# Context projections from undivided fp32 weights and state, and the squares of x summed by ScalarE along its rows

## The chip, the cores and the metric

The kernel runs on one core of a Trainium2 chip. The metric is the time of one execution on the device in microseconds (us), and runs are compared by their medians. A core has a matrix engine (TensorE, in the views PE, with its weight loads as PEld), VectorE (DVE), ScalarE (ACT), GpSimd (POOL) and SyncE (SP), whose queue issues most DMA transfers. Each engine works through its own instructions in order.

## The reference

One layer of a diffusion backbone with 1024 latent tokens and 256 context tokens of width 1024, batch 1. Both streams are normalised and modulated, then projected by the same weights. Of the context only what the latents need is wanted: the forget gates and values of the recurrence, from which its two end states `s_f` and `s_b` come, and the keys and values of two attentions.

```
m_lat = (silu(c) @ w_mod + b_mod).reshape(N_MOD, D);  m_ctx = (silu(c_ctx) @ w_mod + b_mod).reshape(N_MOD, D)
h_lat = rms_norm(x, norm_mix) * (1.0 + m_lat[1]) + m_lat[0]
h_ctx = rms_norm(ctx, norm_mix) * (1.0 + m_ctx[1]) + m_ctx[0]
aq, ak, av, bq, bk, bv, cq, cf, cb, ci, cg, gates = features(h_lat, w_in, qn_b, kn_b, rope)
caq, cak, cav, cbq, cbk, cbv, ccq, ccf, ccb, cci, ccg, cgates = features(h_ctx, w_in, qn_b, kn_b, None)
yc_ctx, s_f, s_b = hgrn2_bidir(ccq, ccf, ccb, cci, ccg, lb_f, lb_b, gn_c, s0, s0)
yc = hgrn2_bidir(cq, cf, cb, ci, cg, lb_f, lb_b, gn_c, s_f, s_b)[0]
ya = window_attn(aq, ak, av, cak, cav, sink_a);  yb = global_attn(bq, bk, bv, cbk, cbv)
x_mix = x + m_lat[2] * merge_branches(ya, yb, yc, gates, w_branch, w_out)
h = rms_norm(x_mix, norm_ffn) * (1.0 + m_lat[4]) + m_lat[3]
out = rms_norm(x_mix + m_lat[5] * conv_ffn(h, w_up, w_dw, b_dw, w_down), norm_final)
```

## The kernel before

The state is kept with channels on the 128 partitions, in KT = 8 tiles of 128 channels. A matmul of full precision is made of three in the format fp32r: a weight tile and a state tile are each divided into a high part (`wh`, `hh`) and a low part (`wl`, `hl`), and `wh*hh + wh*hl + wl*hh` is summed. `w_unit` loads a weight tile of 512 KB into `wr` (SP), casts it to `wh` (ACT) and subtracts to `wl` (DVE, or POOL for the tiles in `CTX_POOL`). Each of these three has three buffers.

The stages are: modulation, context, latent projections of the recurrence (`hgrn_head`, four heads), projections for two attentions, the attentions, and the FFN. This case is about the first 140 us.

*Modulation.* The scale and shift of both streams come in eight groups of 128 channels, each from a tile `wm` of 1 MB. For six groups PE multiplies (`pr`, 8 matmuls with two weight columns, L320), ACT copies the result to `row` and PE turns it (`pm`). Groups 1 and 4 (`MOD_OFF`) are summed on DVE in `acc` (L311, L314). When a group is done, the context tile of the same channels is scaled (`cx`, L252) and divided into `chh` and `chl` (L253, L254). So `ctx_h` runs group by group, and `CTX_K` sets the order of the eight channel tiles inside a context matmul.

*Context.* `ctx_c` makes, for each of four heads, two forget gates (`czf`, `czb`, with `forget` on ACT and DVE into `cF` and `cK`) and the values (`czv`, copied, transposed and copied again into `cV`). `ctx_kv` makes keys and values (`ckv`) of both attentions, with a head norm (`hrsc`) for the second. Beside it runs `lat_norm`: it loads x (`xT`, channels on partitions), squares it on ACT (L369), adds the squares over the channel tiles on POOL and DVE (`xss`), turns the sum on PE (`rcx`, `rms_r`), raises it to -1/2 on POOL (L237), spreads it on PE (`rpx`, `rms_bc`) and finishes the eight latent tiles (`finish_h`: L252 on DVE, L253 on ACT into `hh`, L254 on DVE into `hl`). `weave` puts the steps of the two generators in turn.

*State.* A tree of eight levels multiplies `cK` by the gates from its far side (L452, direction 0 on DVE, direction 1 on POOL by `TREE_POOL`), with the products of neighbours in between (L455). Then PE turns `cK` (`ckp`) and multiplies it by `cV` (`cu`). The first latent projection, `zq`, and the second, `zf`, follow on PE.

The order on each engine is set by a list scheduler at build time from the priorities in the code, so it is a result of the program and not written by hand.

Of the kernel before, what the change touches and what calls it, by code (L numbers as in the profile page):

```python
# [49 lines left out]
NORMAT = 3  # L50
TREE_POOL = (1,)

MOD_OFF = (1, 4)
MOD_FIN = {3: (1,), 6: (4,)}
CTX_K = (0, 2, 1, 3, 5, 4, 6, 7)

# [35 lines left out]
def build(tc, ins, out, dbg=None):  # L92
    nc = tc.nc
    V, A, G, T, SP = nc.vector, nc.scalar, nc.gpsimd, nc.tensor, nc.sync
    with ExitStack() as top:
# [84 lines left out]

        def gemm_cm(psl, w, h, cols, k0=0, c0=0, nk=None, first=True, last=True, order=None):

            wh, wl = w
            hh, hl = h
            nk = nk or wh.shape[1]
            c = slice(c0, c0 + P)
            for n, k in enumerate(order or range(nk)):
                s = first and n == 0
                e = last and n == nk - 1
# [19 lines left out]
        def rms_r(pool, parts, n, name, on_pe):  # L209
# [8 lines left out]
            if on_pe:  # L218

                pc = turned(f"rc{name}")  # L220
                for t in range(nt):
                    for j, ss in enumerate(parts):
                        T.matmul(pc[:, t], ss[:, t * P:(t + 1) * P], ident, start=j == 0, stop=j == len(parts) - 1)
                V.reduce_sum(out=r, in_=pc, axis=AX.X)
            else:
                for g, ss in enumerate(parts):
                    pc = turned(f"rc{name}{g}")
                    for t in range(nt):
                        T.transpose(pc[:, t], ss[:, t * P:(t + 1) * P], ident)
                    if g == 0:  # L230
                        V.reduce_sum(out=r, in_=pc, axis=AX.X)
                    else:
                        r2 = pool.tile([P, nt], F32, tag="rs2", name=f"rs2{name}{g}")
                        V.reduce_sum(out=r2, in_=pc, axis=AX.X)
                        V.tensor_tensor(out=r, in0=r, in1=r2, op=ALU.add)
            V.tensor_scalar(out=r, in0=r, scalar1=1.0 / D, scalar2=EPS, op0=ALU.mult, op1=ALU.add)
            G.tensor_tensor(out=r, in0=r, in1=mhalf[:, :nt], op=ALU.pow)  # L237
            return r
# [17 lines left out]
        with ExitStack() as s0:  # L256
            xp = Aligned(s0.enter_context(tc.tile_pool(name="xp", bufs=1, side="right", reuse_waits="tile")))
            chh = xp.tile([P, KT, LC], F32R, tag="chh", name="chh")
            chl = xp.tile([P, KT, LC], F32R, tag="chl", name="chl")
            xin = s0.enter_context(ExitStack())  # L260
# [5 lines left out]

            hc = (chh, chl)
            units0 = []
# [92 lines left out]
            def lat_norm():  # L361

                xss = [xq.tile([P, L], F32, tag=f"xss{i}", name=f"xss{i}") for i in range(2)]
                for k in range(4):
                    for i in range(2):
                        SP.dma_start(x32[:, 4 * i + k], ins["xT"][(4 * i + k) * P:(4 * i + k + 1) * P, :])
                        xk = x32[:, 4 * i + k]
                        sq = xss[i] if k == 0 else xq.tile([P, L], F32, tag=f"sq{i}", name=f"sqx{k}{i}")
                        A.activation(sq, xk, AF.Square)  # L369
                        if k > 0:  # L370
                            (G if i == 0 else V).tensor_tensor(out=xss[i], in0=xss[i], in1=sq, op=ALU.add)
                    yield
                V.tensor_tensor(out=xss[1], in0=xss[1], in1=xss[0], op=ALU.add)
                rl = rms_row(xq, xss[1:], L, "x")
                yield
                for k in range(KT):
                    finish_h(x32[:, k], rl, a01[:, k, 0:1], m01[:, k, 0, 0:1], hh[:, k], hl[:, k])
                    yield
# [11 lines left out]
            def ctx_unit(nm, h):  # L390
                if units0:
                    return units0.pop(0)
                return w_unit(ins["w_cm"][U_C[nm] + h], KT, P, G if (nm, h) in CTX_POOL else V)

            def ctx_c():
                for h in range(CH):
                    for d, nm in ((0, "f"), (1, "b")):
                        w = ctx_unit(nm, h)
                        z = bank("b", f"cz{nm}{h}", (P, LC))
                        gemm_cm(z, w, hc, slice(0, LC), order=CTX_K)  # L400
                        forget(nc, cp, z, cF[:, d, h], cK[:, d, h], lb[:, d * 4 + h:d * 4 + h + 1],
                               oml[:, d * 4 + h:d * 4 + h + 1], LC, f"c{nm}{h}")
# [42 lines left out]
            while B < LC:  # L445
# [1055 lines left out]
```

## Time and profile before

| | |
|---|---|
| time, median of 3 runs | 2192.55 us (2187.08 to 2196.15) |
| profiled execution | 2193.44 us, its span 2191.7 us |
| busy: PE, PEld, DVE, ACT, POOL | 96%, 79%, 67%, 46%, 20% of the span |
| chain that ended last | PE 22%, DVE 1%, of the span |
| moved by DMA | 224.60 MB, a mean of 102 GB/s |

The span runs from the first to the last instruction; the time of the execution has 1.7 us more around it. Busy shares are means over a long program with stages of different limits, so the first 140 us are read in stretches. A row of a timeline gives start, duration, engine, line, operation, the tile written and those read, and in brackets the idle time of the engine before it with what ended it. An fp32 matmul shows as two records.

### The profile page before, as it was taken

The page shows a single profiled execution, that of the slowest core. Times are in us where ns is not written, and L with a number is a line of the kernel's source. Part 1 is how long each engine was busy: PE and PEld are TensorE (multiplying, and loading weights), DVE is VectorE, ACT ScalarE, POOL GpSimd, SP SyncE. Part 2 cuts the span into 40 slices and gives each one's busy share as a digit, 9 for nine tenths or more (in the row PEclk, how much of TensorE's full clock was granted, in tenths as well). Part 3 has the DMA queues.
Part 4 walks back from the last instruction along what each step waited for, and adds up shares of the span by engine and source line. Part 5 has one row for each costly group of instructions (what it writes and reads, how often), then busy time and mean ns, then how long its engine had stood idle before and what let it go on. Part 6 is the DMA issues. An engine that isn't in the chain of part 4 may idle for free. (4 is left out here: it accounts for less than half of the span.)

```text
span 2191.7 us, 31143 instructions
## 1 busy us (share of the span) xinstructions
PE 2095.4 (96%) x11690; PEld 1737.6 (79%) x11690; DVE 1467.9 (67%) x2593; ACT 1007.5 (46%) x1811; POOL 440.4 (20%) x390
## 2 busy tenths in 40 slices
PE   7789999999999999999999999999999999989997
PEld 3778788889998888877777788877788888768887
DVE  6946566636666687689999856559777777654333
ACT  4523323321122777677777733346444444443322
POOL 1420010001022122132333200012533344100010
PEclk9999999999999999999999999999999999989999
DMA  7420110126653211211110264551322222284343
GB/s 310 129 68 30 49 39 30 54 72 200 199 162 117 90 57 41 80 56 34 30 32 25 94 201 145 176 163 50 104 79 87 82 80 80 87 281 158 108 128 91
DMA packets 94071, 224.60 MB, mean 102 GB/s; under 512 B 10592, under 2 KB 35680, under 8 KB 92896
## 3 DMA queue, kind: packets, MB, share of 16 engines
q1 hardware_dynamic: 93632, 222.55, 31.1%
q8 instruction: 92, 1.51, 0.3%
q14 instruction: 59, 0.48, 0.1%
q10 hardware_dynamic: 288, 0.07, 0.0%
HBM read 176.96 MB, written 45.61 MB: 102 GB/s over the span
## 5 line engine op out<-in xcount | busy, mean ns | idle before, releaser
L176 DVE TENSOR_TENSOR wl<-wr,wh 128x1024 fp32r<-128x1024 f32 x147 | 186.3, 1268 | 250.3 <-ACT wh L175 248.7
L175 ACT CAST wh<-wr 128x1024 fp32r<-128x1024 f32 x152 | 158.6, 1045 | 417.0 <-PE dn L872 83.2
L1244 DVE TENSOR_TENSOR pl<-pp,ph 128x512 fp32r<-128x512 f32 x236 | 158.8, 683 | 9.6 <-ACT ph L1243 8.3
L190 PE MATMUL gz<-hh,wh 128*128 128x512 f32 x384 | 156.4, 408 | 2.9 <-ACT gs L487 2.8
L1243 ACT CAST ph<-pp 128x512 fp32r<-128x512 f32 x236 | 136.2, 584 | 43.7 <-PE pp L1239 40.8
L192 PE MATMUL gz<-hh,wl 128*128 128x512 f32 x384 | 151.9, 396 | 0.0
L191 PE MATMUL gz<-hl,wh 128*128 128x512 f32 x384 | 151.8, 395 | 0.0
L871 PE MATMUL dn<-ac,wh 128*128 128x512 f32 x264 | 103.9, 393 | 11.8 <-ACT ac L646 11.8
L201 PE MATMUL tm<-wl,hh 128*128 128x256 f32 x384 | 108.9, 283 | 2.5 <-DVE wl L176 2.5
L200 PE MATMUL tm<-wh,hh 128*128 128x256 f32 x384 | 108.7, 283 | 0.0
L202 PE MATMUL tm<-wh,hl 128*128 128x256 f32 x384 | 108.6, 283 | 0.0
L1233 PE MATMUL po<-ph,VHL 128*128 128x512 f32 x236 | 104.9, 445 | 1.3 <-ACT ph L1243 1.3
L1234 PE MATMUL po<-pl,VHL 128*128 128x512 f32 x236 | 98.8, 419 | 7.5 <-DVE pl L1244 7.3
L872 PE MATMUL dn<-ac,wh 128*128 128x512 f32 x264 | 103.6, 392 | 0.0
L873 PE MATMUL dn<-ac,wl 128*128 128x512 f32 x264 | 103.4, 392 | 0.0
L1239 PEld LDWEIGHTS pp<-ident,plat 128*128 128x128 f32 x512 | 61.1, 140 | 34.5 <-DVE pl L1244 22.1
L1239 PE MATMUL pp<-ident,plat 128*128 128x128 f32 x512 | 78.2, 275 | 10.3 <-DVE pl L1244 9.3
L190 PEld LDWEIGHTS gz<-hh,wh 128*128 128x128 f32 x384 | 72.8, 190 | 17.2 <-ACT gs L487 5.0
L695 ACT ACTIVATE u<-c,cw 128x1024 f32<-128x1024 f32 x40 | 49.8, 1246 | 76.4 <-DVE c L836 45.3
L192 PEld LDWEIGHTS gz<-hh,wl 128*128 128x128 f32 x384 | 72.5, 189 | 15.4
L191 PEld LDWEIGHTS gz<-hl,wh 128*128 128x128 f32 x384 | 72.8, 190 | 11.6
L781 POOL TENSOR_TENSOR s<-wr 128x512 f32<-128x512 f32 x20 | 30.7, 1534 | 231.7 <-DVE ws2l L647 21.5
(1496 smaller groups left out, 6278.9 us busy)
## 6 DMA issues: line engine op xcount, KB each, us to landing
wr<-in_w_cm SPq DMA_DIRECT2D x56, 512.0 KB, 3.7
wr<-in_w_up SPq DMA_DIRECT2D x44, 512.0 KB, 3.5
wr<-in_w_down SPq DMA_DIRECT2D x33, 512.0 KB, 3.5
wmr<-in_w_mod SPq DMA_DIRECT2D x32, 512.0 KB, 4.6
gate_d<-gs SPq DMA_DIRECT2D x48, 256.0 KB, 2.4
sgt<-gate_d SPq DMA_DIRECT2D x24, 512.0 KB, 3.4
act_d<-u SPq DMA_DIRECT2D x22, 512.0 KB, 2.6
st<-act_d SPq DMA_DIRECT2D x44, 256.0 KB, 4.3
```

The lines of the kernel that those rows point to most:

```text
L175: A.copy(hi[:, :n], raw[:, :n])
L176: (lo_eng or V).tensor_tensor(out=lo[:, :n], in0=raw[:, :n], in1=hi[:, :n].bitcast(F32), op=ALU.subtract)
L190: T.matmul(psl, wh[:, k, c], hh[:, k0 + k, cols], start=s, stop=False)
L191: T.matmul(psl, wh[:, k, c], hl[:, k0 + k, cols], start=False, stop=False)
L192: T.matmul(psl, wl[:, k, c], hh[:, k0 + k, cols], start=False, stop=e)
L200: T.matmul(psl, hh[:, k, toks], wh[:, k % 4, :], start=s, stop=False)
L201: T.matmul(psl, hh[:, k, toks], wl[:, k % 4, :], start=False, stop=False)
L202: T.matmul(psl, hl[:, k, toks], wh[:, k % 4, :], start=False, stop=e)
L1233: T.matmul(po, vv, ph, start=n == 0, stop=False)
L1239: T.transpose(pp[:, h], PT(h, n), ident)
L1243: A.copy(ph, pp)
L1244: V.tensor_tensor(out=pl, in0=pp, in1=ph.bitcast(F32), op=ALU.subtract)
```

## The change

The context's weights and state are no longer divided. `w_raw` loads a weight tile and hands it to PE as it is, in turn in the buffers of `wr`, `wh` and `wl`; the state is one tile `ch` of fp32, and a context matmul is one fp32 matmul for each k. The values are computed with tokens on partitions, so they need no transposes. Modulation group 4 moves from DVE to PE, and the whole tree of the state is on DVE. `lat_norm` loads x a second time, as rows of tokens (`xn`, four buffers): ACT squares a tile and sums along its row in the same instruction (`accum_out`). The sum needs no adding and no turning; the part of `rms_r` behind it becomes `rms_pow`. The tiles of `xT` are loaded behind those of `xn`.

```diff
-CTX_POOL = (('v', 1), ('b', 2), ('v', 2), ('b', 3), ('v', 3))
-TREE_POOL = (1,)
-MOD_OFF = (1, 4)
-MOD_FIN = {3: (1,), 6: (4,)}
-CTX_K = (0, 2, 1, 3, 5, 4, 6, 7)
+MOD_OFF = (1,)
+MOD_FIN = {3: (1,)}
+CTX_K = (0, 2, 1, 3, 4, 5, 6, 7)
...
+        def w_raw(src, nk, ncol):
+            tag, bufs = (("wr", WR), ("wh", WH), ("wl", WL))[cnt[0] % 3]
+            cnt[0] += 1
+            with tc.high_priority(offset=wprio[0]):
+                raw = wp.tile([P, 1024], F32, tag=tag, name=f"{tag}{cnt[0]}", bufs=bufs)
+                SP.dma_start(raw, src)
+            return raw.rearrange("p (k n) -> p k n", k=nk)
...
+            return rms_pow(r)
+        def rms_pow(r):
             V.tensor_scalar(out=r, in0=r, scalar1=1.0 / D, scalar2=EPS, op0=ALU.mult, op1=ALU.add)
-            G.tensor_tensor(out=r, in0=r, in1=mhalf[:, :nt], op=ALU.pow)
+            G.tensor_tensor(out=r, in0=r, in1=mhalf[:, :r.shape[1]], op=ALU.pow)
             return r
...
-                    finish_h(cx[:, k], rc, a01[:, k, 1:2], m01[:, k, 0, 1:2], chh[:, k], chl[:, k])
+                    V.scalar_tensor_tensor(out=cx[:, k], in0=cx[:, k], scalar=a01[:, k, 1:2], in1=rc,
+                                           op0=ALU.mult, op1=ALU.mult)
+                    A.activation(ch[:, k], cx[:, k], AF.Identity, bias=m01[:, k, 0, 1:2])
...
-                    units0.append(w_unit(ins["w_cm"][U_C["fbv"[i - WAT]]], KT, P))
+                    units0.append(w_raw(ins["w_cm"][U_C["fbv"[i - WAT]]], KT, P))
...
-                xss = [xq.tile([P, L], F32, tag=f"xss{i}", name=f"xss{i}") for i in range(2)]
-                for k in range(4):
-                    for i in range(2):
-                        SP.dma_start(x32[:, 4 * i + k], ins["xT"][(4 * i + k) * P:(4 * i + k + 1) * P, :])
-                        xk = x32[:, 4 * i + k]
-                        sq = xss[i] if k == 0 else xq.tile([P, L], F32, tag=f"sq{i}", name=f"sqx{k}{i}")
-                        A.activation(sq, xk, AF.Square)
-                        if k > 0:
-                            (G if i == 0 else V).tensor_tensor(out=xss[i], in0=xss[i], in1=sq, op=ALU.add)
-                    yield
-                V.tensor_tensor(out=xss[1], in0=xss[1], in1=xss[0], op=ALU.add)
-                rl = rms_row(xq, xss[1:], L, "x")
+                nt = L // P
+                rl = xq.tile([P, nt], F32, tag="rs", name="rsx")
+                for t in range(nt):
+                    xn = xq.tile([P, D], F32, tag="xn", name=f"xn{t}", bufs=4)
+                    SP.dma_start(xn, ins["x"][t * P:(t + 1) * P, :])
+                    sq = xq.tile([P, D], F32, tag="sq", name=f"sqx{t}", bufs=2)
+                    A.activation(sq, xn, AF.Square, accum_out=rl[:, t:t + 1])
+                    if t % 2:
+                        yield
+                for k in range(KT):
+                    SP.dma_start(x32[:, k], ins["xT"][k * P:(k + 1) * P, :])
+                rp = rms_bc(rms_pow(rl), L, "x", "b")
...
-                        gemm_cm(z, w, hc, slice(0, LC), order=CTX_K)
+                        for n, k in enumerate(CTX_K):
+                            T.matmul(z, w[:, k], ch[:, k], start=n == 0, stop=n == KT - 1)
...
-                    z = mm2(f"czv{h}")[:, 0, :LC]
-                    gemm_cm(z, w, hc, slice(0, LC), order=CTX_K)
-                    vt = cp.tile([P, LC], F32, tag="vt", name=f"cvt{h}")
-                    A.copy(vt, z)
-                    pt = bank("a", f"cvp{h}", (P, 2, P))
+                    z = bank("a", f"czv{h}", (P, 2, P))
                     for c in range(2):
-                        T.transpose(pt[:, c], vt[:, c * P:(c + 1) * P], ident)
-                    A.copy(cV[:, :, h], pt)
+                        for n, k in enumerate(CTX_K):
+                            T.matmul(z[:, c], ch[:, k, c * P:(c + 1) * P], w[:, k], start=n == 0, stop=n == KT - 1)
+                    A.copy(cV[:, :, h], z)
...
-                        gemm_tm(z, ws, hc, slice(tt * P, (tt + 1) * P))
+                        for k in range(KT):
+                            T.matmul(z, ch[:, k, tt * P:(tt + 1) * P], ws[k // 4][:, k % 4], start=k == 0,
+                                     stop=k == KT - 1)
...
-                    (G if d in TREE_POOL else V).tensor_tensor(out=K_, in0=K_, in1=F_, op=ALU.mult)
+                    V.tensor_tensor(out=K_, in0=K_, in1=F_, op=ALU.mult)
```

On PE, from the last turning of group 3 (`pm3`) to the first gate of the context. `pr` are the modulation groups, `czv0`, `czf0` and so on the context projections. Before:

```order
L284 MATMUL pm3_272<-ident_89,row3_195 128x2 x2
L190 MATMUL czv0_445<-chh_111,wh3_238 128x256
L191 MATMUL czv0_445<-chl_112,wh3_238 128x256
L320 MATMUL pr5_261<-wm5_259,scc_83 2x256 x8
L192 MATMUL czv0_445<-chh_111,wl3_239 128x256
L190 MATMUL czv0_445<-chh_111,wh3_238 128x256
L191 MATMUL czv0_445<-chl_112,wh3_238 128x256
L192 MATMUL czv0_445<-chh_111,wl3_239 128x256
L320 MATMUL pr6_282<-wm6_280,scc_83 2x256 x8
```

And now:

```order
L292 MATMUL pm3_237<-ident_89,row3_186 128x2 x2
L330 MATMUL pr4_226<-wm4_222,scc_83 2x256 x8
L292 MATMUL pm4_257<-ident_89,row4_235 128x2 x2
L330 MATMUL pr5_246<-wm5_244,scc_83 2x256 x8
L330 MATMUL pr6_266<-wm6_264,scc_83 2x256 x8
L292 MATMUL pm5_277<-ident_89,row5_255 128x2 x2
L330 MATMUL pr7_286<-wm7_284,scc_83 2x256 x8
L292 MATMUL pm6_297<-ident_89,row6_275 128x2 x2
L292 MATMUL pm7_302<-ident_89,row7_295 128x2 x2
L411 MATMUL czf0_340<-ch_111,wr1_155 128x256 x8
L411 MATMUL czb0_363<-ch_111,wh2_175 128x256 x8
L419 MATMUL czv0_385<-wl3_224,ch_111 128x128 x16
```

The values of head 0 stood between the groups of the modulation; now the whole modulation comes first, with group 4 in it, and the context follows in whole units.

On SP, the queue of transfers behind the last small load of the modulation (`gnc`). `wr4` and so on are weight tiles of 512 KB (now named by the buffer that holds them), `x32` is the tile of `xT`. Before:

```order
L341 DMA gnc_92<-in_gn 128x1
L366 DMA x32_117<-in_xT 128x1024 x4
L172 DMA wr4_484<-in_w_cm 128x1024
L366 DMA x32_117<-in_xT 128x1024 x2
L172 DMA wr5_528<-in_w_cm 128x1024
L366 DMA x32_117<-in_xT 128x1024 x2
L172 DMA wr6_587<-in_w_cm 128x1024
```

And now:

```order
L377 DMA xn0_355<-in_x 128x1024
L377 DMA xn1_359<-in_x 128x1024
L185 DMA wr4_411<-in_w_cm 128x1024
L377 DMA xn2_377<-in_x 128x1024
L377 DMA xn3_381<-in_x 128x1024
L185 DMA wh5_435<-in_w_cm 128x1024
L377 DMA xn4_403<-in_x 128x1024
L377 DMA xn5_407<-in_x 128x1024
L377 DMA xn6_427<-in_x 128x1024
L377 DMA xn7_431<-in_x 128x1024
L185 DMA wl6_470<-in_w_cm 128x1024
L383 DMA x32_116<-in_xT 128x1024 x8
```

The eight tiles of `xT` stand behind eight tiles of `xn`, the last four of which each wait for a square.

On ACT, the end of the context stage now, from the last gate of head 3 to the copies of the state. `wh17` to `wh19` are casts of weights for the latent projections `zq`, `zf` and `zb`, `hsqc` squares for the head norm, `ckt` and `st_ctx` copies in the state's chain.

```order
L978 ACTIVATE snegcf3_565<-czf3_556 128x256
L979 ACTIVATE cF_338<-czf3_556 128x256
L173 CAST wh17_794<-wr17_792 128x1024
L978 ACTIVATE snegcb3_584<-czb3_575 128x256
L979 ACTIVATE cF_338<-czb3_575 128x256
L420 COPY cV_339<-czv3_594 128x2x128
L173 CAST wh18_855<-wr18_853 128x1024
L434 COPY ckvs00_628<-ckv00_619 128x256
L434 COPY ckvs01_640<-ckv01_631 128x256
L173 CAST wh19_915<-wr19_913 128x1024
L987 ACTIVATE hsqc0_660<-ckv10_650 128x128
```

Before, the same stretch held the casts of `wh13` to `wh16` too, and those of `wh17` to `wh19` stood between the squares `hsqc0` and `hsqc1` and behind them; now two of the three stand ahead of the copies that free the banks of `ckv`, and all three ahead of `hsqc0`.

## Rows read from the trace of the kernel before

**Rows 1.** The page, busy time, share of the span and instructions of each engine.

```profile
PE 2095.4 (96%) x11690; PEld 1737.6 (79%) x11690; DVE 1467.9 (67%) x2593; ACT 1007.5 (46%) x1811; POOL 440.4 (20%) x390
```

**Rows 2.** Busy time by stretch of the span: start and end in us, length, then busy time (and instructions) of PE, PEld, DVE, ACT and POOL, granted clock of PE, busy share of the DMA engines, GB/s.

```profile
40.00:60.00 20.00, 19.06 (x131) 15.12 (x130) 16.01 (x30) 16.10 (x25) 6.83 (x3) 1.00 0.41 147
60.00:80.00 20.00, 13.36 (x94) 12.74 (x93) 16.65 (x14) 7.28 (x13) 7.90 (x5) 0.83 0.29 98
80.00:100.00 20.00, 16.02 (x121) 14.93 (x120) 19.97 (x20) 12.76 (x20) 12.05 (x4) 0.98 0.39 119
100.00:120.00 20.00, 15.99 (x98) 14.71 (x98) 16.49 (x24) 7.90 (x12) 7.95 (x7) 0.85 0.45 142
120.00:138.00 18.00, 15.29 (x88) 12.08 (x87) 7.29 (x11) 4.51 (x13) 6.00 (x4) 1.00 0.24 73
138.00:200.00 62.00, 62.00 (x435) 50.78 (x435) 33.69 (x45) 20.65 (x28) 0.00 (x0) 1.00 0.14 43
```

**Rows 3.** Timeline of PE around the end of the context stage: `ckp` is the turned tree, `zf` the second latent projection.

```profile
111.76 0.40 PE L191 MATMUL zf<-hl,wh 128*128 128x512 f32 x1
...
127.05 0.52 PE L462 MATMUL ckp<-ident,cK 128*128 128x128 f32 x3 [2.41 <-DVE cK L452]
...
137.69 0.39 PE L192 MATMUL zf<-hh,wl 128*128 128x512 f32 x1
...
137.92 0.39 PE L190 MATMUL zf<-hh,wh 128*128 128x512 f32 x1
```

**Rows 4.** Waits of PE from 40 to 140 us: who waited for what, us in total, times, longest.

```profile
PE rcx L229 <- DVE xss L373: 6.0, 1, 6.0
PE zq L192 <- DVE wl L176: 4.0, 1, 4.0
```

**Rows 5.** Timeline of PE in the modulation.

```profile
20.12 0.28 PE L284 MATMUL pm<-ident,row 2*128 2x2 f32 x2 [0.45 <-ACT row L322]
...
20.93 3.62 PE L320 MATMUL pr<-wm,scc 128*2 128x256 f32 x16
...
25.42 0.28 PE L284 MATMUL pm<-ident,row 2*128 2x2 f32 x2
...
28.97 6.22 PE L320 MATMUL pr<-wm,scc 128*2 128x256 f32 x16
```

**Rows 6.** Slices of 1 us, columns as in rows 2.

```profile
27.00:28.00 1.00, 0.00 (x0) 0.00 (x0) 1.00 (x4) 1.00 (x2) 0.00 (x0) 0.72 1.06 442
...
99.00:100.00 1.00, 1.00 (x7) 1.00 (x6) 1.00 (x2) 0.37 (x1) 1.00 (x1) 0.56 0.77 238
```

**Rows 7.** The modulation's weights, tile `wm`: the last issues on SP's queue in the timeline, the matmuls that read it (ns, min/median/max), and the landing of its eight transfers.

```profile
10.55 5.80 SPq L301 DMA_DIRECT2D wm<-in_w_mod  x3
...
L320 PE MATMUL pr<-wm,scc x96: 377/379/631, 8.0 to 45.5; 128*2 128x256 f32 x96
...
DMA to landing us min/median/max: 5.3/14.3/16.8
```

**Rows 8.** Timeline of PE, two stretches of matmuls one behind the other: fp32r with 256 columns, the first and the last of 19; and fp32 with 128 weights and 128 columns (`o`, two records each).

```profile
47.17 0.28 PE L191 MATMUL czf<-chl,wh 128*128 128x256 f32 x1
...
49.32 0.28 PE L191 MATMUL czf<-chl,wh 128*128 128x256 f32 x1
...
217.12 0.38 PE L1116 MATMUL o<-ST,QQ 128*128 128x128 f32 x2
...
218.91 0.28 PE L1115 MATMUL o<-ST,QQ 128*128 128x128 f32 x1
```

**Rows 9.** Groups by line from 180 to 260 us, weight loads of 128x128, fp32 (`kt`) and fp32r (`wh`): busy time in us, mean of one in ns.

```profile
L1102 PEld LDWEIGHTS u<-Vt,kt 128*128 128x128 f32 x28 | 3.4, 191 | 0.9 <-ACT kt L1099 0.8
...
L190 PEld LDWEIGHTS zf<-hh,wh 128*128 128x128 f32 x16 | 3.0, 189 | 0.4
```

**Rows 10.** Squares on ACT, and the reading of an accumulator after another activation of 128x1024 (ns, min/median/max).

```profile
L369 ACT ACTIVATE sqx<-x x6: 1040/1052/1107, 44.0 to 58.3; 128x1024 f32<-128x1024 f32 x6
...
L1355 ACT ACTIVATION_READ_ACCUMULATOR plat<-sbl,st__9186 x4: 189/195/215, 943.1 to 951.7; 128x1 f32 x4
```

**Rows 11.** Timeline of POOL and DVE: the power of the norm, the latent rows (L252, L254), a forget gate and its successor (L970 to L254), the tree (L452) and its products (L455).

```profile
71.28 1.65 POOL L237 TENSOR_TENSOR rsx<-rsx,mhalf 128x8 f32<-128x8 f32 x1 [5.98 <-DVE rsx L236]
...
77.82 1.27 DVE L252 SCALAR_TENSOR_TENSOR x<-x,a,rpx 128x1024 f32<-128x1024 f32 x1
79.01 1.28 DVE L254 SCALAR_TENSOR_TENSOR hl<-x,m,hh 128x1024 fp32r<-128x1024 f32 x1
...
84.18 0.34 DVE L970 TENSOR_SCALAR cK<-snegcb,lbs 128x256 f32<-128x256 f32 x1
...
84.84 1.27 DVE L254 SCALAR_TENSOR_TENSOR hl<-x,m,hh 128x1024 fp32r<-128x1024 f32 x1
...
107.52 0.68 DVE L452 TENSOR_TENSOR cK<-cK,cF 128x512 f32<-128x512 f32 x1
108.13 1.22 DVE L455 TENSOR_TENSOR cF<-cF 128x1024 f32<-128x1024 f32 x1
```

**Rows 12.** Weight tiles from 60 to 135 us: cast on ACT, low half on DVE (ns, min/median/max), and the landing of their transfers.

```profile
L175 ACT CAST wh<-wr x14: 1028/1050/1069, 59.2 to 111.4; 128x1024 fp32r<-128x1024 f32 x14
...
L176 DVE TENSOR_TENSOR wl<-wr,wh x9: 1210/1214/1337, 68.3 to 121.7; 128x1024 fp32r<-128x1024 f32 x9
...
DMA to landing us min/median/max: 3.4/3.6/5.1
```

More of the change, by code (lines that the diff above doesn't have):

```diff
@@ L179, in w_unit, with gemm_cm @@
                     lo[:, :n].rearrange("p (k n) -> p k n", k=nk))
-        def gemm_cm(psl, w, h, cols, k0=0, c0=0, nk=None, first=True, last=True, order=None):
+        def w_raw(src, nk, ncol):
[5 more added lines that the diff above has]
+            return raw.rearrange("p (k n) -> p k n", k=nk)
+        def gemm_cm(psl, w, h, cols, k0=0, c0=0, nk=None, first=True, last=True):
             wh, wl = w
@@ L186, in gemm_cm @@
             c = slice(c0, c0 + P)
-            for n, k in enumerate(order or range(nk)):
-                s = first and n == 0
-                e = last and n == nk - 1
+            for k in range(nk):
+                s = first and k == 0
+                e = last and k == nk - 1
                 T.matmul(psl, wh[:, k, c], hh[:, k0 + k, cols], start=s, stop=False)
@@ L257, in build @@
             xp = Aligned(s0.enter_context(tc.tile_pool(name="xp", bufs=1, side="right", reuse_waits="tile")))
-            chh = xp.tile([P, KT, LC], F32R, tag="chh", name="chh")
-            chl = xp.tile([P, KT, LC], F32R, tag="chl", name="chl")
+            ch = xp.tile([P, KT, LC], F32, tag="ch", name="ch")
             xin = s0.enter_context(ExitStack())
@@ L265, in build @@
             xm_ = Aligned(xw.enter_context(tc.tile_pool(name="xm_", bufs=1)))
-            hc = (chh, chl)
             units0 = []
@@ L361, in lat_norm @@
             def lat_norm():
-                xss = [xq.tile([P, L], F32, tag=f"xss{i}", name=f"xss{i}") for i in range(2)]
-                for k in range(4):
-                    for i in range(2):
-                        SP.dma_start(x32[:, 4 * i + k], ins["xT"][(4 * i + k) * P:(4 * i + k + 1) * P, :])
-                        xk = x32[:, 4 * i + k]
-                        sq = xss[i] if k == 0 else xq.tile([P, L], F32, tag=f"sq{i}", name=f"sqx{k}{i}")
-                        A.activation(sq, xk, AF.Square)
-                        if k > 0:
-                            (G if i == 0 else V).tensor_tensor(out=xss[i], in0=xss[i], in1=sq, op=ALU.add)
-                    yield
-                V.tensor_tensor(out=xss[1], in0=xss[1], in1=xss[0], op=ALU.add)
-                rl = rms_row(xq, xss[1:], L, "x")
+                nt = L // P
[10 more added lines that the diff above has]
+                rp = rms_bc(rms_pow(rl), L, "x", "b")
                 yield
                 for k in range(KT):
-                    finish_h(x32[:, k], rl, a01[:, k, 0:1], m01[:, k, 0, 0:1], hh[:, k], hl[:, k])
+                    finish_h(x32[:, k], rp, a01[:, k, 0:1], m01[:, k, 0, 0:1], hh[:, k], hl[:, k])
                     yield
@@ L392, in ctx_unit @@
                     return units0.pop(0)
-                return w_unit(ins["w_cm"][U_C[nm] + h], KT, P, G if (nm, h) in CTX_POOL else V)
+                return w_raw(ins["w_cm"][U_C[nm] + h], KT, P)
             def ctx_c():
@@ L417, in ctx_kv @@
                 for br in range(2):
-                    ws = [w_unit(ins["w_tm"][(br * 3 + 2) * 2 + kh], 4, 256) for kh in range(2)]
+                    ws = [w_raw(ins["w_tm"][(br * 3 + 2) * 2 + kh], 4, 256) for kh in range(2)]
                     for tt in range(2):
                         z = bank("b", f"ckv{br}{tt}", (P, 256))
-                        gemm_tm(z, ws, hc, slice(tt * P, (tt + 1) * P))
+                        for k in range(KT):
+                            T.matmul(z, ch[:, k, tt * P:(tt + 1) * P], ws[k // 4][:, k % 4], start=k == 0,
+                                     stop=k == KT - 1)
                         kv = cp.tile([P, 256], F32, tag="ckvs", name=f"ckvs{br}{tt}", bufs=2)
@@ L1434, in prepare @@
     r["xT"] = np.ascontiguousarray(i["x"][0].T)
+    r["x"] = np.ascontiguousarray(i["x"][0])
     r["ctxT"] = np.ascontiguousarray(i["ctx"][0].T)
```

## The prediction, made before the changed kernel was run

> **What bounds the kernel now.** The page comes first: TensorE (PE) is busy 96% of the span [rows 1], and the chain that ended last is PE work, with DVE at 1%. An average hides where the missing part lies, so I cut the span into stretches. From 138 to 200 us PE is busy 62.00 of 62.00 us at the full clock; before that, from 40 to 138 us, its busy times add up to 79.7 of 98 us, and in two of the stretches the granted clock is 0.83 and 0.85 [rows 2]. So the change, which touches only the context stage and the norm of x ahead of it, is worth what it moves the moment at which PE stops waiting and works through the latent projections. That moment is the projection `zf`, at 137.69 us [rows 3]. All that comes after is PE's and moves with it.
>
> The waits of PE say why the stage is slow now [rows 4]: 6.0 us for the sum of squares of x (`xss`, added on DVE and POOL) and 4.0 us for `wl`, the low half of a weight, made by DVE; the smaller ones are for DVE too. PE waits for DVE, which is busy 19.97 of 20 us from 80 to 100 [rows 2]. The long waits are also followed by stretches at the lower clock, so they are paid once more.
>
> **The change, part by part.** Three things happen. PE gets more work; DVE, ACT and POOL get less; and the order on PE becomes one row of long groups.
>
> *Modulation.* Group 4 goes from DVE to PE. One such group (16 records, fp32) takes 3.62 us at the full clock and 6.22 at the half one [rows 5]. PE order is now `pr4` to `pr7` with nothing of the context between them, so they start where `pm3` ends, at 25.7 (25.42 + 0.28): 4 x 3.62 = 14.5, four times 0.45 for the copy of a row by ACT, two exposed `pm` of 0.28: 2.4. The first context matmul starts at 25.7 + 14.5 + 2.4 = 42.6 us. Its modulation weights are there: the last is issued by 16.4 us (10.55 + 5.80) and takes at most 16.8 to land [rows 7], 33.2, and `pr7` asks for it near 38.
>
> *Context matmuls.* In the kernel before there are three fp32r matmuls of 256 columns for each k, 18 steps of them in 2.15 us (47.17 to 49.32), 0.1194 each [rows 8]: 384 of them, 45.9 us. After it is one fp32 matmul, which the trace shows as two records. No fp32 matmul with 128 weights and 256 columns is in the trace. From one side, `o` has fp32 weights of 128x128 and 128 columns: eight pairs of records start within 1.79 us (217.12 to 218.91) [rows 8], 0.224 a matmul, 0.112 a record. From the other side, a `pr` has 256 columns and two weights: 3.62 / 16 = 0.226 a record at most [rows 5], and without the 0.38 of the last one [rows 7], 3.24 / 15 = 0.216. The 0.112 says that full weights cost a record little beyond its columns; I take 0.219 for a record, 0.438 for a matmul, between 0.432 and 0.452. So 64 matmuls for `f` and `b` and 32 for `ckv` take 96 x 0.438 = 42.0; the 64 for `v` have 128 columns: 64 x 0.224 = 14.3. The sum is 56.4 us, 10.5 more than now: on PE itself this part of the change costs. The transposes of `v` (eight) go, and so do those of `xss`; those that spread `r` (`rpx`, 0.85) stay. From 42.6 this is 42.6 + 56.4 + 0.85 = 99.9 us, if nothing stops PE.
>
> *What could stop it.* The squares: eight on ACT at 1.05, with 0.19 for reading the accumulator [rows 10], 10 us in all; they need `xn`, of which 4 to 7 wait for a free buffer, that is for squares 0 to 3 (about 39 to 46 us, since ACT stands in order behind the copies of `row6` and `row7`). The last square follows `czb0` and ends near 53; with 1.65 us of POOL [rows 11] `rsx` is there at 55. PE asks for it after `czb1`, at 42.6 + 4 x 3.5 + 3.6 = 60.2. So the second load and the squares lie under 5 us of cover. The 8 x 512 KB of `xT` stand behind them on SP's queue from 46 us; at the 442 GB/s of a stretch in which DMA was the limit [rows 6] that is 9.5 us, 56 to 58 with the weight ahead of them, again just ahead of need. If that cover were gone it would cost what is late, one for one.
>
> *DVE.* Off the engines go the splits of 16 weight tiles: 16 casts at 1.05 on ACT, 11 lows at 1.21 on DVE [rows 12], five on POOL; and on DVE eight `chl`, the sums of `xss` and the products of group 4. What is left is a chain. It starts on the latent rows at 61.3. There are 16 operations 1.19 apart (77.82 to 79.01), four pairs for the forget gates at 0.66 (84.18 to 84.84), the tree: now all 16 multiplications 0.61 apart, and products of 1.13 falling to 0.1, 2.6 together [rows 11]; two `wl` at 1.21 [rows 12]. In sum 61.3 + 19.0 + 2.6 + 9.8 + 2.6 + 2.4 = 97.7, with 1.2 for waiting on the last `hh`, 0.9 of small operations and 0.8 for POOL's power of `hrsc` in between: 100.6. DVE and PE meet within a microsecond.
>
> *Tail.* From `ckp` to `zf` it is 10.6 us now (127.05 to 137.69) with 17 matmuls of `zq` in it; 31 had been done earlier [rows 3]. After the change all 48 come behind `ckp`: 31 x 0.23 = 7.1 more. New is a wait: the second `cu` needs the bank of `ckv11`, which ACT frees only after DVE's `wl19` (1.21) and the small chain of `hrsc1`; about 1.8 us, with all of PE behind it. So `zf` starts at 100.6 + 10.6 + 7.1 + 1.8 = 120.1 us. Two of its 48 matmuls are done early now (the row at 111.76 is the second), 0.45. Gain: 137.7 - 120.1 - 0.45 = 17.1. From 100 to 120 us the granted clock is 0.85 now [rows 2], a loss of 20 x 0.15 = 3.0 us in two stretches at the half rate, each a little behind a wait (the first begins in the slice at 99, 0.56 [rows 6]): 1.5 for one. I count half of that for the new wait, 0.8. That leaves 16.3 us.
>
> The profiled execution took 2193.44 us (span 2191.7 and 1.7 around it), 0.9 above the median of 2192.55. 2193.44 - 16.3 = 2177.1: **2177 us**, 0.7% under the median. Under 0.5%, about 11 us, a measurement of this kernel can't be told from no change.
>
> **Rivals.**
> *The clock stays low in the modulation.* `pr` matmuls have two weight columns. The clock fell at about 27.4 us (0.72 in that slice) [rows 6], after a pause of matmuls from 25.7, and `pr5`, from 28.97, took 6.22 [rows 5]: nearly all of it at the low rate. If such groups don't hold the clock, `pr4` to `pr7` cost up to 4 x 2.6 = 10.4 more, and the gain is 6 to 11 us (2182 to 2187). Against it: `pr3` at 20.93 ran in 3.62 [rows 5]. The Trainium skill (TensorE: Matmul & The Clock Gate, What's actually happening) says that the low rate is the default and that activity releases it; by that, four groups in a row keep the high rate, which the trace bears out for `pr3` alone.
>
> *The weights of the latents are late.* `wr17` waits for `czf3` (78 us), `wr18` for DVE's `wl17`, `wr19` for `wl18`; ACT casts each in order, with `hsqc0` behind. A link is 3.6 + 1.05 + 1.21 us [rows 12]. By the medians the third cast ends at 96, where `ckv10` also ends. At the longest landing (5.1) it is 4.5 us later, and the tail with it: gain 12, 2181.
>
> *Slower: the fp32 weight loads are not hidden.* If each of 320 records paid its load of 0.19 us, that is 61 us more: 2238. It decides from 16.3 / 320 = 0.05 us per record. Against it: an fp32 load of 128x128 is listed at 0.191 us [rows 9], yet such matmuls run 0.112 apart [rows 8], so the loads overlap. The same page (Weight-path perf modes — Fast Weight Load (FWL) and DoubleRow) states that the fast weight load is off for FP32, which would make exactly these loads the slow ones. Here an fp32r load (0.189) and an fp32 load (0.191) take the same time [rows 9], so the measurement decides.
>
> *No effect.* The gain is given back after `zf`, by DVE in the first head. PE at 62.00 of 62.00 speaks against it. 2188 to 2196.
>
> **How the numbers follow.** My forecast 0.60 (2172 to 2182), the clock 0.15, late weights 0.12, no effect 0.06, slower 0.07. Faster by more than 11 us: the forecast, the late weights and a little of the clock, 0.74. Within: 0.19. Slower: 0.07. The range leaves out the last two cases: 2171 (a record at 0.213, no loss of clock, and a tail without the wait) to 2187.
>
> **What would show it.** `czf0` starts near 42.6, later than 47 means the first rival; fp32 matmuls of 256 columns 0.44 apart; no wait of PE for `rpx` at 60; `ckv11` done near 100 and `ckp` within 1 us of it; a wait at the second `cu`; `zf` near 120. I am wrong if records are 0.27 or more apart, if PE stands still between `czf0` and `ckp` for more than 5 us, or if PE after `zf` waits for DVE more than now.

## The result, and the profile after

The changed kernel took 2176.82 us (median of 4 runs, 2173.61 to 2178.01), the kernel before 2192.94 us beside it: a ratio of 0.9928, with a 95% interval of 0.9908 to 0.9949. A second series gave 2174.07 us (5 runs, 2173.05 to 2175.31) beside 2189.02 for the kernel before, 0.9929 [0.9915, 0.9943]; one run of the kernel before in it took 5305.5 us and isn't counted in the ratio. So it is faster by 0.7%, and the forecast was 2177 us, 0.7%.

The profiled execution took 2173.61 us, its span 2171.8 us. The page's busy row, which answers [rows 1]:

```profile
PE 2090.0 (96%) x11624; PEld 1733.7 (80%) x11624; DVE 1425.7 (66%) x2560; ACT 992.8 (46%) x1800; POOL 405.9 (19%) x374
```

PE's share is 96% as before: the mean doesn't show the change. The stretches do, with columns as in [rows 2]:

```profile
20.00:40.00 20.00, 18.48 (x89) 7.42 (x90) 6.25 (x27) 6.68 (x13) 0.72 (x1) 1.00 0.97 391
40.00:60.00 20.00, 19.70 (x109) 16.77 (x108) 3.97 (x13) 12.46 (x27) 1.64 (x1) 1.00 0.83 304
60.00:80.00 20.00, 19.65 (x127) 18.12 (x126) 19.43 (x21) 10.06 (x14) 0.00 (x0) 1.00 0.76 303
80.00:100.00 20.00, 19.90 (x108) 17.61 (x106) 18.17 (x32) 6.85 (x13) 0.59 (x1) 1.00 0.34 118
100.00:120.00 20.00, 17.59 (x96) 14.17 (x97) 3.63 (x10) 4.79 (x15) 1.19 (x2) 1.00 0.25 77
```

From 40 to 100 us PE now stands still for 0.75 us in all, and the granted clock (the column behind the five engines) is 1.00 everywhere, where it was 0.83 and 0.85 in two stretches of [rows 2]. PE's four longest waits from 15 to 140 us, for [rows 4]:

```profile
PE pr L330 <- DMA wm<-in_w_mod: 2.1, 1, 2.1
PE cu L478 <- ACT ckvs L441: 1.5, 1, 1.5
PE pm L292 <- ACT row L332: 1.3, 3, 0.5
PE ckp L472 <- DVE cK L462: 1.1, 2, 0.9
```

The 6.0 us for `xss` and the 4.0 us for `wl` are gone. And PE's timeline at the places that the prediction named:

```profile
42.43 3.72 PE L411 MATMUL czf<-ch,wr 128*128 128x256 f32 x16
...
59.92 1.04 PE L257 MATMUL rpx<-ident,rsx 128*128 128x128 f32 x8
...
87.65 1.89 PE L430 MATMUL ckv<-wh,ch 128*128 128x256 f32 x8
89.37 1.89 PE L430 MATMUL ckv<-wr,ch 128*128 128x256 f32 x8
...
98.01 1.89 PE L430 MATMUL ckv<-wr,ch 128*128 128x256 f32 x8
100.08 0.52 PE L472 MATMUL ckp<-ident,cK 128*128 128x128 f32 x3 [0.19 <-DVE cK L462]
101.47 0.77 PE L472 MATMUL ckp<-ident,cK 128*128 128x128 f32 x5 [0.87 <-DVE cK L462]
...
104.65 0.71 PE L478 MATMUL cu<-cV,ckt 128*128 128x128 f32 x4 [1.46 <-ACT ckvs L441]
...
120.08 0.39 PE L197 MATMUL zf<-hh,wh 128*128 128x512 f32 x1
```

`zf` starts at 120.08 us, where it started at 137.69 [rows 3]. The first row of the projection behind it, `zb`, is free of the two matmuls done early. It moved by 17.16 us. Before, then after:

```profile
148.12 0.39 PE L190 MATMUL zb<-hh,wh 128*128 128x512 f32 x1
```

```profile
130.96 0.39 PE L197 MATMUL zb<-hh,wh 128*128 128x512 f32 x1
```

The first gate projection behind the four heads (`gz`) started at 423.47 us and now at 406.33: 17.14 us, so nothing was given back there. Near the end, at `rcf`, it is 19.88 us (2065.97 to 2046.09). The other 2.7 us I do not put down to the change. In two stretches far behind it the execution of before fell to the lower clock, 3.0 us lost in these three rows by what the clock lacks (columns as above), and that of after stayed at 1.00 in the same work:

```profile
620.00:630.00 10.00, 8.00 (x35) 6.34 (x34) 5.08 (x15) 3.08 (x6) 2.24 (x2) 0.91 0.53 162
630.00:640.00 10.00, 10.00 (x65) 9.15 (x64) 4.89 (x9) 1.92 (x3) 1.01 (x1) 0.92 0.33 95
...
1440.00:1450.00 10.00, 7.65 (x29) 5.89 (x28) 10.00 (x15) 9.97 (x16) 0.00 (x0) 0.87 0.23 59
```

In a second profile of the changed kernel the clock did fall in the later of the two places (0.90 from 1420 to 1430 us), so it is not bound to the kernel before. From `zf` to the end of the span it took 2054.0 us before and 2051.7 after, and in the eleven other profiled executions below between 2049.9 and 2055.6, in no order that follows the edits. So the experiments are read at the start of `zf`, and in time only where there are several runs. `zf` scatters too: two profiles of the changed kernel have it at 120.08 and 120.42 us, two of the version with an early copy (below) at 117.34 and 119.11. A difference of under 2 us between single profiles shows little by itself.

### The profile page after: what moved, and what is told of

Its sections match the earlier page's. It is cut to its first block, busy times and chain, and to the rows that moved or that the text cites. A ratio compares the mean times of both kernels' runs of the same rounds, so it can differ in the third digit from the quotient of the medians.

```text
span 2171.8 us, 30945 instructions
## 1 busy us (share of the span) xinstructions
PE 2090.0 (96%) x11624; PEld 1733.7 (80%) x11624; DVE 1425.7 (66%) x2560; ACT 992.8 (46%) x1800; POOL 405.9 (19%) x374
## 5 line engine op out<-in xcount | busy, mean ns | idle before, releaser
L174 DVE TENSOR_TENSOR wl<-wr,wh 128x1024 fp32r<-128x1024 f32 (+1 forms) x136 | 170.7, 1255 | 253.9 <-ACT wh L173 248.0
L173 ACT CAST wh<-wr 128x1024 fp32r<-128x1024 f32 (+1 forms) x136 | 142.0, 1044 | 417.6 <-PE dn L882 80.2
L208 PEld LDWEIGHTS tm<-wl,hh 128*128 128x128 f32 x384 | 73.7, 192 | 3.1 <-DVE wl L174 2.7
```

Source lines behind the costliest of these rows:

```text
L173: A.copy(hi[:, :n], raw[:, :n])
L174: (lo_eng or V).tensor_tensor(out=lo[:, :n], in0=raw[:, :n], in1=hi[:, :n].bitcast(F32), op=ALU.subtract)
L208: T.matmul(psl, hh[:, k, toks], wl[:, k % 4, :], start=False, stop=False)
```

## Experiments

**One part undone at a time.** The old norm in the changed kernel:

```diff
...
-                    SP.dma_start(xn, ins["x"][t * P:(t + 1) * P, :])
...
-                    A.activation(sq, xn, AF.Square, accum_out=rl[:, t:t + 1])
...
+                        SP.dma_start(x32[:, 4 * i + k], ins["xT"][(4 * i + k) * P:(4 * i + k + 1) * P, :])
...
+                        A.activation(sq, xk, AF.Square)
...
+                            (G if i == 0 else V).tensor_tensor(out=xss[i], in0=xss[i], in1=sq, op=ALU.add)
...
```

> The changed kernel with the norm of before: x is loaded once, its squares are added over the channel tiles on POOL and DVE, turned and reduced. Nothing else is undone. Theory A (the weights' and the state's division was what DVE had too much of; with DVE free the old norm is nearly as good): the adding ends near 55 us, under the cover of czf1 and czb1, but the turning (rcx, 0.9 us), DVE's reduction and POOL's power (1.6 us) stand behind czb1 on PE, so rpx and the latent rows on DVE start about 3 us later than the 61.2 us of the changed kernel, and zf starts at about 123 us (122 to 124.5) where it now starts at 120.1. Rival (the new norm carries the gain, since PE waited 6.0 us for the sum before the change): PE waits 5 us or more for rcx again and zf starts at 126 us or later. A second rival (the doubled load costs as much as it gives, since the transfers run at 0.95 to 1.03 from 50 to 70 us): zf at 120 us or earlier.

Measured: `zf` at 121.37 us, 1.3 later (2173.65 us, one run). PE's timeline:

```profile
60.44 1.04 PE L236 MATMUL rcx<-ident,xss 128*128 128x128 f32 x8
...
64.94 1.09 PE L257 MATMUL rpx<-ident,rsx 128*128 128x128 f32 x8 [1.68 <-POOL rsx L247]
...
102.24 0.58 PE L197 MATMUL zq<-hh,wh 128*128 128x512 f32 x1
...
105.74 1.24 PE L472 MATMUL ckp<-ident,cK 128*128 128x128 f32 x8 [1.54 <-DVE hrsc L991]
```

The norm is 5.0 us later at `rpx` and `ckp` 5.7 us later, more than expected, yet `zf` loses less than expected. Two things make up for it. Seven matmuls of `zq` now stand ahead of `ckp` in PE's order (the row of `zq` is the first) and fill 1.6 of the 3.1 us between `ckv11` and `ckp`; and behind `ckp` PE no longer waits, where the changed kernel waits 0.87 and 1.46 us. The norm doesn't carry the gain, so the first rival is out. The second (the load costs what it gives, `zf` at 120 or earlier) missed by 1.3 us, of which 0.5 are there already at `czf0` (42.95 us, 42.43 in the changed kernel), ahead of the norm: what the new norm is worth in the changed kernel lies within the scatter.

Group 4 of the modulation back on DVE:

```diff
-MOD_OFF = (1,)
-MOD_FIN = {3: (1,)}
+MOD_OFF = (1, 4)
+MOD_FIN = {3: (1,), 6: (4,)}
```

> The changed kernel with modulation group 4 back on DVE; nothing else is undone. The changed kernel's DVE is busy 6.25 of 20 us from 20 to 40 us, and PE 18.48. Theory A (from the modulation to ckp PE itself is the limit, so each us taken from PE comes out at zf): PE loses 16 records of 3.61 us and 0.5 us of waiting for a row, gains a turning of 0.66; czf0 starts near 38.7 us instead of 42.4 and zf near 116.9 us (116.4 to 117.8) instead of 120.1. Rival (the transfers are the limit: their share is 0.97 from 20 to 40 us and about 1.0 from 54 to 70): czf0 starts early, but PE then waits for weights or rows of x and zf stays within 1 us of 120.1.

Measured: `zf` at 122.23 us, 2.1 later instead of 3.2 earlier (2176.74 us, one run). My theory fell, and so did the rival as I had put it, since the wait comes ahead of `czf0` and not behind it. PE's timeline:

```profile
25.21 0.28 PE L292 MATMUL pm<-ident,row 2*128 2x2 f32 x2
27.39 5.30 PE L330 MATMUL pr<-wm,scc 128*2 128x256 f32 x16 [1.91 <-DMA wm<-in_w_mod]
34.66 5.30 PE L330 MATMUL pr<-wm,scc 128*2 128x256 f32 x16 [1.96 <-ACT row L332]
```

```profile
28.00:30.00 2.00, 2.00 (x6) 0.65 (x5) 2.00 (x6) 0.00 (x0) 0.00 (x0) 0.50 1.03 430
```

Without group 4 PE runs out of work at 25.5 us, because the weights of group 5 haven't landed; the clock falls to 0.50, falls again behind a second wait of 1.96 us, and two groups take 5.30 us instead of 3.61. `czf0` starts at 46.29. So the move of group 4, which I had counted as PE work alone, fills a hole. It stands where the kernel before had a hole too, after which `pr5` took 6.22 us [rows 5]; there the profile puts the wait down to a cast on ACT (`wh` of `czv0`, which stood ahead of `pr5`).

Half of the tree back on POOL:

```diff
-                    V.tensor_tensor(out=K_, in0=K_, in1=F_, op=ALU.mult)
+                    (G if d == 1 else V).tensor_tensor(out=K_, in0=K_, in1=F_, op=ALU.mult)
```

> The changed kernel with direction 1 of the state's tree back on POOL; nothing else is undone. Theory A: DVE loses 8 multiplications of 0.61 us, but POOL needs 1.14 to 2.0 us for each (median 1.88 in the kernel before) from about 86.4 us, so that the tree ends at 99 to 102 us, as now, and the powers of the head norm stand behind it on POOL, so that the second cu gets its bank about 0.9 us later: zf at 120.0 to 122 us. Rival (DVE's tree sets the end, and relieving it lets ckp start as soon as ckv11 is through): zf at 119.3 us or earlier.

Measured: `zf` at 125.34 us, 5.3 later (2177.19 us, one run), far outside what I expected. DVE's timeline, the products of neighbours of the tree's later levels and the last multiplication, first with the tree on POOL, then in the changed kernel:

```profile
92.11 1.37 DVE L465 TENSOR_TENSOR cF<-cF 128x256 f32<-128x256 f32 x1
...
94.13 1.19 DVE L465 TENSOR_TENSOR cF<-cF 128x128 f32<-128x128 f32 x1
...
98.71 1.04 DVE L465 TENSOR_TENSOR cF<-cF 128x32 f32<-128x32 f32 x1
...
101.45 0.69 DVE L462 TENSOR_TENSOR cK<-cK,cF 128x512 f32<-128x512 f32 x1
```

```profile
92.76 0.42 DVE L465 TENSOR_TENSOR cF<-cF 128x256 f32<-128x256 f32 x1
...
94.43 0.28 DVE L465 TENSOR_TENSOR cF<-cF 128x128 f32<-128x128 f32 x1
...
97.42 0.18 DVE L465 TENSOR_TENSOR cF<-cF 128x32 f32<-128x32 f32 x1
...
100.73 0.68 DVE L462 TENSOR_TENSOR cK<-cK,cF 128x512 f32<-128x512 f32 x1
```

DVE has eight multiplications less and still ends 0.7 us later: while POOL works on its half, a product of 128x32 takes 1.04 us instead of 0.18. The waits behind that (1.62 us for `cK`, 1.08 for a bank) then cost the clock. PE's first `ckp`, and stretches of 2 us, with the tree on POOL:

```profile
102.29 0.52 PE L472 MATMUL ckp<-ident,cK 128*128 128x128 f32 x3 [1.62 <-DVE cK L462]
```

```profile
102.00:104.00 2.00, 1.42 (x9) 1.22 (x9) 1.16 (x4) 0.00 (x0) 1.74 (x2) 0.81 0.03 8
104.00:106.00 2.00, 1.53 (x6) 1.03 (x5) 1.93 (x5) 0.92 (x3) 0.00 (x0) 0.50 0.19 66
...
112.00:114.00 2.00, 2.00 (x11) 1.86 (x10) 0.00 (x0) 0.75 (x2) 0.00 (x0) 0.63 0.00 0
```

**Alone, and in pairs.** Three kernels: undivided weights and state alone (the three parts above undone at once), the same with group 4 on PE (`norm_tree`), and the new norm alone in the kernel before.

> Undivided weights and state alone: the changed kernel with the norm of before, group 4 on DVE and half of the tree on POOL, all three undone at once. One by one they moved zf from 120.1 to 121.4 (norm), 122.2 (group 4, by a hole in PE at 25.5 us and the half clock behind it) and 125.3 us (tree, by waits at 100 us and the half clock behind them). Theory A (the division was the load that mattered, the three others are additions): zf at 123.5 to 129 us, that is at least half of the 17 us. Rival (the parts need each other): zf at 131 us or later.

> The changed kernel with the norm of before and half of the tree on POOL, group 4 still on PE. All three undone together moved zf by 11.9 us (120.1 to 132.0), more than the sum of the three alone (1.3 + 2.1 + 5.3 = 8.7). Theory A (the norm and the tree need each other: with the old norm alone seven matmuls of zq stand ahead of ckp in PE's order and fill its wait, with the tree on POOL as well they stand behind it, so a later tree is a bare wait and the clock falls): zf at 128.5 to 131 us. Rival (what is missing lies between group 4 and one of the two): zf at 126 to 127.5 us, the sum of the two alone.

> The new norm alone: the kernel before with x loaded a second time as rows and its squares summed by ACT (three buffers xn and one for the squares here, for lack of room); weights and state divided as before. Theory A (DVE's divisions are the limit from 80 us on, and the wait of 6.0 us for the sum hides part of them): the wait at rcx goes, but DVE saves only six or so of 1.2 us, and other waits for DVE grow; zf at 131 to 135 us instead of 137.7. Rival (each us of the wait is a us at the end, and the stretch at the half clock goes with it): zf at 130 us or earlier. Second rival (the doubled transfer holds the weights up): zf at 137 us or later.

Measured, the start of `zf` in PE's timeline of each, in this order:

```profile
131.99 0.39 PE L197 MATMUL zf<-hh,wh 128*128 128x512 f32 x1
```

```profile
127.47 0.39 PE L197 MATMUL zf<-hh,wh 128*128 128x512 f32 x1
```

```profile
135.12 0.39 PE L190 MATMUL zf<-hh,wh 128*128 128x512 f32 x1
```

The times are 2185.98, 2181.11 and 2191.24 us (one run each). Undivided weights alone give 5.7 of 17.6 us (0.45 of both are the two matmuls that the kernel before had done early): a third, not half, so my theory fell there and its rival came, `zf` at 131 us or later. The steps add up in one order: undivided 5.7 (137.69 to 131.99), group 4 on PE 4.5 (to 127.47), the tree off POOL 6.1 (to 121.37), the new norm 1.3 (to 120.08). These shares hold for this order; undivided weights put on last, on top of the other three, were not run. Norm and tree do not need each other (127.47 is 7.4 behind, and 1.3 + 5.3 is 6.6), so that theory fell as well. Group 4 is worth more where the others are undone (4.5) than in the changed kernel (2.1). The traces show two reasons: without it `czf0` starts 4.6 us later there (47.22 and 42.65) and 3.9 later here, and here the later PE is spared the waits that the changed kernel has at `czf2`, the gate of head 2 (0.35), and at `ckp` (0.19 and 0.87).

The new norm alone gains 2.6 us (2.1 without those two early matmuls), although the wait for `xss` is gone; that is at the edge of what I expected. PE's waits in it show two others in its place:

```profile
PE czf L190 <- ACT wh L175: 6.8, 1, 6.8
PE ckv L201 <- DVE wl L176: 6.7, 1, 6.7
```

With the weights divided, the wait taken from PE came back as waits for divided weights.

**The wait that is left.** In the changed kernel the second `cu` waits 1.46 us for a bank that `ckv11` holds until the head norm is through. Here ACT copies the whole of `ckv10` and `ckv11` at once, and the head norm works on the copy:

```diff
-                            rs = head_rms(nc, cp, z[:, :128], 2, f"c{tt}", mhalf)
...
+                            A.copy(kv, z)
+                            rs = head_rms(nc, cp, kv[:, :128], 2, f"c{tt}", mhalf)
...
-                            A.copy(kv[:, 128:], z[:, 128:])
```

> The changed kernel, but ACT copies the whole of ckv10 and ckv11 out of their banks at once, and the head norm works on the copy. So the bank that the second cu needs is free when ckv11 has been copied, and no longer when the chain of the head norm is through. Theory A: the wait of 1.46 us of PE at the second cu goes, zq and the rest move up, zf starts at about 118.7 us (118.4 to 119.2). Rival (ckt on ACT, or the tree on DVE, releases the second cu a little later anyway): zf within 0.4 us of 120.1.

> The changed kernel with ACT copying ckv10 and ckv11 out of their banks at once, timed in five rounds. In its one look zf started at 117.3 us instead of 120.1. Theory A (what zf gains arrives at the end): 2.7 us less than the changed kernel's 2176.8, so 2174.1 us, a ratio of 0.9915 to the kernel before. Rival (given back later): 0.9928 as the changed kernel.

Measured: `zf` at 117.34 us, 2.7 earlier, and 119.11 in the second profile, where PE had reached the context 1.2 us later (`czf0` at 44.02). Four runs: 2171.93 us, 0.9918 [0.9904, 0.9931]. The timeline of the first shows `cu` in one piece:

```profile
100.14 1.31 PE L471 MATMUL ckp<-ident,cK 128*128 128x128 f32 x8
...
101.75 1.09 PE L477 MATMUL cu<-cV,ckt 128*128 128x128 f32 x8
```

The gain is larger than the wait, since the two waits of `ckp` on DVE (0.19 and 0.87) are gone as well. The ratio lies 0.0010 below that of the changed kernel, 2.2 us, which these two intervals can't tell apart.

**A group that can go to DVE.** If the hole was what spoke against group 4, a later group should do: by then PE has `pr4` and `pr5` to work on. This one stands on top of the early copy.

```diff
-MOD_OFF = (1,)
-MOD_FIN = {3: (1,)}
+MOD_OFF = (1, 6)
+MOD_FIN = {3: (1,), 7: (6,)}
```

> As the one before it, and with modulation group 6 on DVE (instead of PE), its turning behind group 7. Group 4 on DVE had made a hole in PE at 25.5 us, since the weights of group 5 hadn't landed, and the clock fell. Group 6 is late enough that pr4 and pr5 fill PE until its weights are there, and DVE is busy 6.6 of 20 us from 20 to 40. Theory A: no hole, no half clock; pr7 starts near 34.0 us, the first context matmul near 38.5 instead of 42.8, zf at 113.3 to 115 us, and 2171 us in time, a ratio of 0.990. Rival 1 (the weights of group 7 land later than 34 us): PE waits, the clock falls and zf is at 117 us or later. Rival 2 (the transfers of weights and x behind it are the limit): PE waits between czf0 and ckp for what it gained ahead.

Measured: `zf` at 115.67 us, 2173.08 us, 0.9919 [0.9906, 0.9933]. There is no hole, and the context starts at 39.17 us. But PE then waits, as the second rival had it. (The second profile of the changed kernel has a wait of 1.1 us at the same place, without this move.)

```profile
PE czf L411 <- DMA wr<-in_w_cm: 2.2, 1, 2.2
```

Of the time nothing arrived (2171.93 us without this move, in the same series): in this profile the way from `zf` to the end was the longest of all, 2055.6 us. Next I raised the priority of the context's weights, so that two of them go ahead of `xT` on SP's queue:

```diff
-WPRIO_C = 30
+WPRIO_C = 60
```

> The version with the early copy of ckv and group 6 on DVE, with a higher priority of the context's weights (60 instead of 30), so that the weights of czf2 and czb2 stand ahead of the tiles of xT on SP's queue. In the version before it PE waited 2.2 us at czf2 for its weights. Theory A (the order of the transfers, not their sum): the wait goes and zf starts at 113 to 114 us instead of 115.7. Rival (the sum of the bytes is the limit: the wait moves to xT, and DVE starts on the latents as much later): zf at 115 us or later. Time: what came after zf took 2050 to 2056 us in the runs so far, so 2167 with a range of 2163 to 2171 us.

> The changed kernel itself again, unchanged, beside the versions of this call and on the same chip: a ratio of 0.9928 to the kernel before as at first, zf at 120.1 us within 2 us, and 2050 to 2056 us from there to the end.

Measured: the wait is gone and `zf` starts at 113.60 us, so it was the order of the transfers and not their sum. This version took 2168.49 us (4 runs, 2167.62 to 2171.46), 0.9905 [0.9891, 0.9919]; the changed kernel beside it took 2174.07 (2173.05 to 2175.31), with `zf` at 120.42. The ranges of the two don't meet: 5.6 us less in time, 6.8 at `zf`. It beats both kernels.

## Why the prediction was right, point by point

- *PE is the limit, and `zf` is the place to look.* Right: the shift at `zb` is 17.16 us, at `gz` 17.14; 17.1 was forecast. That `zf` came within 0.02 us (120.08, forecast 120.1) is luck: `ckp` began at 100.08 and not at 100.6, and from there to `zf` it took 20.0 us and not 19.5. One reading of the waits of before was wrong: the smaller ones are not all for DVE, 1.4 us was for a `wl` of POOL and 0.7 for a cast on ACT.
- *Modulation, 42.6 us for the first context matmul.* 42.43. The granted clock was 1.00 throughout, so the first rival did not come: four groups in a row hold the clock. With group 4 on DVE it did fall, behind a hole of 1.91 us. My sum was right, but it did not see that group 4 was also the cover of that hole, worth 2.1 us.
- *A record at 0.219 us.* Two groups of 8 records start 1.72 us apart (87.65 to 89.37): 0.215, below my bounds by a thousandth. Each record's weight load took 0.190 us in this stretch (the group of `czb`'s loads below), and fits beside it: the slow rival is out. By the rule of the Trainium skill (TensorE: Matmul & The Clock Gate, Weight-path perf modes — Fast Weight Load (FWL) and DoubleRow), under which FP32 gets no fast load, the loads might have shown; the trace has them at 0.190 and hidden. `ckv11` ended at 99.90 us, forecast 99.9.

```profile
L411 PEld LDWEIGHTS czb<-ch,wh 128*128 128x128 f32 x64 | 12.2, 190 | 1.7
```

- *Squares and the second load.* The last square ended at 52.8 and POOL's power at 54.75 (55 forecast), by its row in POOL's timeline below, and PE asked at 59.92 (60.2). The cover of 5 us was there. The tiles of `xT` came later than forecast (the last was issued at 52.9 us and none took less than 7.4 to land, so past 60 and not by 58), but DVE did not wait for them. The weights behind them were left out of the forecast: in the second profile PE waits 1.1 us for those of `czf2`. What failed is the sentence that losing the cover costs "what is late, one for one": the old norm was 5.0 us late at `rpx` and cost 1.3.

```profile
53.11 1.64 POOL L247 TENSOR_TENSOR rsx<-rsx,mhalf 128x8 f32<-128x8 f32 x1 [31.03 <-DVE rsx L246]
```

- *DVE and PE meet within a microsecond.* DVE's tree ended at 101.41 (100.6 forecast), PE's `ckv11` at 99.90; PE waited 0.19 and 0.87 us.
- *The wait at the second `cu`.* Forecast 1.8, measured 1.46, with the cause as named: taking it away gave 2.7 us.
- *0.8 us for the clock behind that wait.* This term failed. The clock stayed at 1.00. Half was a bet between two cases, and no run shows half: here the clock did not fall, and with waits of 1.62 and 1.08 us in the same place (tree on POOL) it did, and the way from `ckp` to `zf` took 23.1 us instead of 20.0.
- *Span.* 2177.1 was forecast for an execution with the tail of before; this one took 2173.61, 0.8 less by the clock term and 2.7 less because its tail was free of two falls of the clock. The medians (2176.82 and 2174.07) lie between the two.
- *Where the gain comes from.* Here the total was right and the picture wrong in part. I told it as DVE's relief from dividing. By the runs, in the one order in which the parts were added, that is 5.7 us; group 4 on PE (4.5) and a tree that POOL doesn't touch (6.1) are worth as much or nearly, since one closes a hole behind which the clock fell and the other frees DVE of POOL.

## What to carry to other kernels

Follow one instruction behind which the bottleneck engine never waits again, and sum up to its start: it told 17.1 us where medians of whole runs scatter by three or four. An engine that is moved work may be paid for it: ask not only what the work costs there, but which hole it fills, and which engine it stops disturbing. And a late input can cost less than its lateness: with the old norm `ckp` came 5.7 us later and `zf` 1.3, since PE's order had put seven matmuls of `zq` ahead of `ckp` and two later waits went.

## What the runs showed of the hardware

DVE operations with two inputs slow down while POOL works on SBUF: products of 128x32 from 0.18 to 1.04 us, of 128x128 from 0.28 to 1.19. With the old norm the same is seen at an addition of 128x1024, 2.54 us beside POOL's additions and 1.21 without. The Trainium skill (GPSIMD Engine Reference, Specifications) states that the two share their SBUF interfaces, with contention for DVE instructions with two SBUF inputs (or in a 2-port perf mode); the trace agrees. The price is not a fixed one: by POOL's rows with the tree on POOL, its operations end at 93.20, 95.17 and 99.71 us, and the three slow products that DVE began beside them (DVE's first timeline in that experiment) end at 93.48, 95.32 and 99.75. Each lasted until 0.04 to 0.28 us behind the end of POOL's operation. POOL's rows, and then DVE's additions with the old norm:

```profile
91.61 1.59 POOL L462 TENSOR_TENSOR cK<-cK,cF 128x512 f32<-128x512 f32 x1 [0.69 <-DVE cF L465]
93.63 1.54 POOL L462 TENSOR_TENSOR cK<-cK,cF 128x512 f32<-128x512 f32 x1 [0.43 <-DVE cF L465]
...
98.21 1.50 POOL L462 TENSOR_TENSOR cK<-cK,cF 128x512 f32<-128x512 f32 x1 [0.83 <-DVE cF L465]
```

```profile
50.08 2.54 DVE L381 TENSOR_TENSOR xss<-xss,sqx 128x1024 f32<-128x1024 f32 x1 [1.06 <-ACT sqx L379]
...
55.31 1.21 DVE L381 TENSOR_TENSOR xss<-xss,sqx 128x1024 f32<-128x1024 f32 x1
```

PE's clock stayed at full rate behind waits of 0.87 and 1.46 us in the changed kernel, and fell to 0.50 behind one of 1.91 us (group 4 on DVE) and behind 1.62, 0.29, 0.47 and 1.08 us in a row (tree on POOL). The length of a wait alone does not decide it: it stayed at 1.00 also behind 2.1 us for `wm` in the changed kernel (the `pr` behind it, at 15.90, took 3.61 us), behind 2.2 us at `czf2` with group 6 on DVE, and behind 2.41 us at `ckp` in the kernel before ([rows 3]; 1.00 from 120 to 138 us in [rows 2]).
